# Products of the second layer's modulation tied to the VectorE split of a later weight unit, at most two pending

## The chip, the cores and the metric

The kernel runs on one core of one Trainium2 chip. The metric is the device time of one execution in microseconds (us). TensorE does the matrix products, VectorE and ScalarE work on tiles element by element, GpSimd does little here, and SyncE (SP) does nothing but issue the DMA loads of the weights.

## What is computed

A network of two layers on 256 rows of 2048 numbers, all in fp32. Each layer scales, shifts and gates with a modulation that is a product of one vector with a large matrix. The first layer's mixer is gated linear attention with a short convolution, the second's is a windowed mean with a grouped projection. Cut to what matters here:

```python
def modulation(cond, w, b, n):
    m = jax.nn.silu(cond) @ w[:, :n * D_MODEL] + b[:n * D_MODEL]
    return jnp.split(m, n, axis=-1)

for i in range(DEPTH):                                    # DEPTH = 2
    sh, sc, gt = modulation(c_lat, w_ada[i], b_ada[i], 3) # w_ada[i]: 2048 x 6144
    u = x * (1.0 + sc) + sh
    ...
    y = even_mixer(u @ w_in_e[j], ..., w_out_e[j]) if i % 2 == 0 else odd_mixer(u @ w_in_o[j], ..., w_out_o[j])
    x = layer_norm(alpha * x + gt * y, ln_g[i], ln_b[i])
```

## The kernel before

**Weights.** All weights are read once, as units of 1 MB (four tiles of 128 rows by 512 columns; `load_unit`, line 138). SyncE issues the loads one after another, and every one of them takes the next of four buffers named `raw`. So a load is issued only when what was in that buffer four loads earlier has been used. A unit is then split in two halves (`split_unit`): ScalarE casts each half to the high part `wh` (line 152), VectorE subtracts it from the raw value to get the low part `wl` (line 153). Four halves of each are kept, and some units ("wide" ones) have halves of their own, `swh` and `swl`. Each product of the network is three matmuls (lines 190 to 192): high by high, high by low, low by high. `w_next` keeps loads two units ahead of the unit in use and splits one unit ahead.

**Modulation.** The modulation's matrix (`w_ada`) comes through the same four buffers, also 1 MB at a time. The second layer's share, and the first layer's gate `gt`, are made on VectorE beside the first layer's products: for each 1 MB load four instructions (`ada_accum`, lines 532 and 534) multiply a 128x512 tile by one number of each partition and add it into a row of sums, `aacc`. When four loads are done (16 instructions), TensorE sums `aacc` over the partitions (`adaS`, line 555, or `gtb`, line 521), and VectorE adds the bias (lines 293 and 295). Such a load with its products is called a modulation load below, and the four instructions its products.

**What sets the order.** These loads and products are written by Python generators. `tick` is called for every weight unit and gives the generators a credit (so many steps per unit, a number for each stage), and `pump_ada` spends it, one `yield` per step: mostly a load with its four products. Whatever is not done when the kernel needs it is written out at once: `cols_ab` calls `pump_ada(1000)` in front of the last column block of the first layer's output projection, since the second layer's input u1 needs the whole scale and shift (A1, B1). The remaining 16 loads, those of the second layer's gate, come in the second layer. Products carry a priority; among what is ready to be placed, the scheduler orders each engine by priority, and each engine then runs its instructions in that order.

**The end of the first layer.** The output projection (`ln_blocks`) goes through four blocks of 512 columns, each with four weight units, called q0 to q3 here. Of the last block, q2 and q3 are wide. Its sums are `oacc`, one for the upper 128 rows (m=0) and one for the lower (m=1). When a half of the rows is complete, VectorE multiplies by the gate (`arow`), adds it to `xr`, takes statistics and normalises (lines 1086 to 1100 and 1156), TensorE transposes, ScalarE applies A1 and B1 (line 1164) and casts (`u1h`, line 1167), and the second layer's products (`xacc`) follow.

Of the kernel before, what the change touches and what calls it, by code (L numbers as in the profile page):

```python
# [9 lines left out]
F32 = mybir.dt.float32  # L10
# [3 lines left out]
ALU = mybir.AluOpType  # L14
# [46 lines left out]
def kernel(  # L61
# [24 lines left out]
    nc = tc.nc  # L86
    names = {}

    def nm(s):
        names[s] = names.get(s, 0) + 1  # L90
        return f"{s}_{names[s]}"
# [9 lines left out]
    @contextmanager  # L101
    def prio(offset):
        old = tc.cur_priority
        tc.cur_priority = max(0, old + offset)
        start = tc.cur_priority
        yield
        tc.cur_priority = old + tc.cur_priority - start
# [4 lines left out]
    def slot(shape, dt=F32, name="s"):  # L112
        return s4p.tile(shape, dt, tag="s4", name=nm(name))

    def mp(shape, name="mp"):
        return mpp.tile(shape, F32, tag="mp", name=nm(name))

    def acc_bank(name="acc"):
        return accp.tile([P, 512], F32, tag="acc", name=nm(name))
# [6 lines left out]
    def small(shape, name):  # L126
        return smp.tile(shape, F32, tag=name, name=nm(name))
# [15 lines left out]
    def split_unit(r, nk, wide=False):  # L143
        parts = []
        for j in range(0, nk, 2):
            w = min(2, nk - j)
            if wide:
                h, l = slot([P, w, 512], F32R, "swh"), slot([P, w, 512], F32R, "swl")
            else:
                h = whp.tile([P, w, 512], F32R, tag="wh", name=nm("wh"))  # L150
                l = wlp.tile([P, w, 512], F32R, tag="wl", name=nm("wl"))
            nc.scalar.copy(h, r[:, j : j + w, :])  # L152
            nc.vector.tensor_tensor(out=l, in0=r[:, j : j + w, :], in1=h.bitcast(F32), op=ALU.subtract)  # L153
            for i in range(w):
                parts.append((h[:, i, :], l[:, i, :]))
        return parts
# [5 lines left out]
    wst = {"l": 0, "s": 0, "u": 0}  # L162
    wraws, wparts = {}, {}

    def w_ahead(nl, ns):
        top = len(specs)
        while wst["s"] < min(top, wst["u"] + ns):
            w_load(wst["s"] + 1)
            i = wst["s"]
            with prio(-SPLIT_PRIO if n0_done[0] else -SPLIT_PRIO0):  # L170
                wparts[i] = split_unit(wraws.pop(i), specs[i][2], i in wide)
            wst["s"] = i + 1
        w_load(min(top, wst["u"] + nl))

    def w_load(n):
        while wst["l"] < n:
            i = wst["l"]
            wraws[i] = load_unit(*specs[i])
            wst["l"] = i + 1
# [136 lines left out]
    k0 = 0  # L316
# [153 lines left out]

    def pump_ada(n):
        while n > 0 and ada_bg:
            try:
                next(ada_bg[0])
                n -= 1
            except StopIteration:
                ada_bg.pop(0)

    def ada_unit(layer, k0, n0):

        if not ADA_SLOT:
            r = load_unit(w_ada[layer], k0, 4, n0)
            return [r[:, j, :] for j in range(4)]
        q = {"s": nc.sync, "g": nc.gpsimd}[ADA_SLOT]
        parts = []
        for k in (k0, k0 + 2):
            r = slot([P, 2, 512], F32, "araw")
            q.dma_start(r, w_ada[layer][k * P : (k + 2) * P, n0 : n0 + 512].rearrange("(k p) n -> p k n", p=P))
            parts += [r[:, 0, :], r[:, 1, :]]
        return parts  # L490
# [16 lines left out]
    def ada_rows_gen(layer, dst, engs):  # L507

        for nb in range(4):
            if nb % 2 == 0:  # L510
                dst.append(slot([P, 2, 512], F32, "gt"))
            g = dst[nb // 2][:, nb % 2, :]
            n0 = 2 * D + nb * 512
            nc.gpsimd.dma_start(g, b_ada[layer : layer + 1, n0 : n0 + 512].to_broadcast([P, 512]))
            a = small([P, 512], "aacc1")
            for k0 in range(0, KT, 4):
                ada_accum(ada_unit(layer, k0, n0), k0, a, engs)
                if k0 == KT - 4:
                    yield
                    pb = mp([P, 512], "gtb")  # L520
                    nc.tensor.matmul(out=pb, lhsT=ones, rhs=a, start=True, stop=True)
                    nc.vector.tensor_tensor(out=g, in0=pb, in1=g, op=ALU.add)
                    gt_done.setdefault(id(dst), set()).add(nb)
                yield

    def ada_accum(r, k0, a, engs):
        e = engs[(k0 // 4) % len(engs)]
        with prio(ADA_PRIO):
            for j in range(4):
                sc = sil[:, k0 + j, 2:3]  # L530
                if k0 + j == 0:
                    e.tensor_scalar(out=a, in0=r[j], scalar1=sc, scalar2=None, op0=ALU.mult)
                else:
                    e.scalar_tensor_tensor(out=a, in0=r[j], scalar=sc, in1=a, op0=ALU.mult, op1=ALU.add)  # L534

    def ada_cols_gen(layer, n0, dst, bias, one, engs, on_pe=()):

        for nb in range(4):
            ns = slice(4 * nb, 4 * nb + 4)
            if nb in on_pe:  # L540
                hold = []
                for _ in ada_acc_gen(layer, n0 + nb * 512, hold):
                    if not hold:
                        yield
                add_bias(dst[:, ns], to_cols(hold[0], 512)[:, :, 0], bias[:, ns], one)
                yield
                continue
            a = small([P, 512], "aacc1")
            for k0 in range(0, KT, 4):
                ada_accum(ada_unit(layer, k0, n0 + nb * 512), k0, a, engs)  # L550
                yield
            yield
            pt = mp([P, 4], "adaS")
            for q in range(4):
                nc.tensor.matmul(out=pt[:, q : q + 1], lhsT=a[:, q * P : (q + 1) * P], rhs=ones[:, 0:1], start=True, stop=True)
            add_bias(dst[:, ns], pt, bias[:, ns], one)
# [9 lines left out]
    prev, k0 = None, 0  # L566
# [31 lines left out]
    def drain(gen=None):  # L598
        while bg and (gen is None or gen in bg):
            pump(1e9 if gen is None else 1)  # L600
# [460 lines left out]
    for i in range(2):  # L1061
        n0 = i * 512
# [13 lines left out]
    def ln_blocks(src, order, getu, res, gt, budget, after, before=None, between=None, halves=False):  # L1076

        rt, accs, seen = {}, {}, {}

        def add(nb, m, cs=slice(0, 512)):  # L1080
            if nb not in rt:
                rt[nb] = res(nb)
            while ada_bg and not (len(gt) > nb // 2 and nb in gt_done.get(id(gt), ())):
                pump_ada(1)
            t = small([P, 512], "arow")[:, cs]
            nc.vector.tensor_tensor(out=t, in0=accs[nb][m + (cs.start > 0)][:, cs], in1=gt[nb // 2][:, nb % 2, cs], op=ALU.mult)
            r = rt[nb][:, m, cs]
            nc.vector.scalar_tensor_tensor(out=r, in0=r, scalar=ALPHA, in1=t, op0=ALU.mult, op1=ALU.add)
            parts = [r] if not (halves and m) or cs != slice(0, 512) else [r[:, 0:256], r[:, 256:512]]
            for v in parts:  # L1090
                nc.vector.bn_stats(out=cst[m][:, seen_st[m], :], in_=v)
                seen_st[m] += 1

        def done(m, cs, end):
            with prio(-LN_PRIO if m else 0):
                add(order[-1][0], m, cs)
                if not end:
                    return
                mv = small([P, 2], "mv")
                nc.vector.bn_aggr(out=mv, in_=cst[m][:, 0 : seen_st[m], :])  # L1100
                after(m, rt, mv[:, 0:1], mv[:, 1:2])

        seen_st = [0, 0]
        for nb, qs in order[:-1]:
            if 1 in qs:
                drain()
            if nb not in accs:
                accs[nb] = [acc_bank("oacc") for _ in range(2)]
                seen[nb] = 0
            gemm(src, nb * 512, qs, range(2), getu, accs[nb], first=seen[nb] == 0, last=seen[nb] + len(qs) == 4, budget=budget)  # L1110
            seen[nb] += len(qs)
            if seen[nb] == 4:
                for m in range(2):
                    add(nb, m)
        if before:
            before()
        nb, qs = order[-1]
        accs[nb] = [acc_bank("oacc") for _ in range(2)]
        gemm_by_tile([(src, nb * 512, qs, accs[nb], True)], getu, done, between=between, halves=halves)
        return rt  # L1120
# [181 lines left out]
    for s in ODD:  # L1302
        g = int(s[1])
        if s == "g0":
            accs = [acc_bank("xacc") for _ in range(2)]
            f = gate_evac(0)
# [81 lines left out]
```

## Time and profile before

| | |
|---|---|
| time, median of 3 runs | 1006.15 us (1005.88 to 1007.38) |
| time of the profiled execution | 1010.29 us |
| its span | 1008.5 us |
| TensorE busy | 960.9 us (95%) |
| TensorE weight loads | 759.2 us (75%) |
| VectorE busy | 801.6 us (79%) |
| ScalarE busy | 469.3 us (47%) |
| DMA | 252 GB/s over the span |

The span is the profiled execution from its first to its last instruction. Busy shares are means over all stages. A wait names what the waiting instruction got last; the engine behind it in the list waits with it, since each engine runs its own list in order.

### The profile page before, as it was taken

To read this page: it belongs to the slowest core of one execution; us is meant where nothing else is said; L and a number is where in the kernel's file an instruction comes from. 1 tells how busy PE (TensorE), PEld (TensorE's weight loads), DVE (VectorE), ACT (ScalarE), POOL (GpSimd) and SP (SyncE) were. 2 spreads that over 40 slices of the span, in tenths; PEclk is the share of its full clock that TensorE was granted. 3 is DMA by queue.
4 is the path that set the end of the run, shared out by engine and by line. 5 is a ranking of instruction groups with operands and counts; after the bars stand their busy time and mean duration, and the time that the engine had idled before them with its cause. 6 is when DMAs were issued, how large, how long until landed. Compare 5 with 4: busy or idle time off the path is not lost.

```text
span 1008.5 us, 14323 instructions
## 1 busy us (share of the span) xinstructions
PE 960.9 (95%) x5654; PEld 759.2 (75%) x5654; DVE 801.6 (79%) x1142; ACT 469.3 (47%) x643; POOL 24.4 (2%) x56
## 2 busy tenths in 40 slices
PE   5899999999999999999999899999999999989995
PEld 4566656778878877887878778888778778778885
DVE  1555546979996999779999688897979997666676
ACT  2422214356675676236454344445745555435340
POOL 2000000000000000000000000000010001000000
PEclk9999999999999999999999999999999999999998
DMA  9977889566787586867767877985497999875532
GB/s 265 329 263 262 276 284 336 193 243 231 258 302 252 188 269 219 257 206 274 241 228 234 284 255 247 353 298 207 152 368 275 304 334 322 278 266 203 174 119 83
DMA packets 150371, 255.44 MB, mean 253 GB/s; under 512 B 5078, under 2 KB 46720, under 8 KB 150304
## 3 DMA queue, kind: packets, MB, share of 16 engines
q1 hardware_dynamic: 146592, 245.13, 72.4%
q0 software_dynamic: 2896, 8.72, 2.7%
q10 hardware_dynamic: 816, 0.68, 0.3%
q8 instruction: 44, 0.72, 0.3%
q14 instruction: 23, 0.19, 0.0%
HBM read 252.41 MB, written 2.10 MB: 252 GB/s over the span
## 4 chain that ended last, share of the span: by engine, by line
PE 41%; DVE 33%; DMA 18%; issue 5%; ACT 3%; SPq 0%; DVEq 0%; ACTq 0%
DMA raw<-in_w_ada_dram 15%; DVE wl L153 11%; DVE aacc L534 9%; PE oacc L191 5%; PE oacc L192 5%; PE oacc L190 5%; DMA raw<-in_w_in_o_dram 3%; PE xacc L192 3%; PE xacc L191 3%; PE xacc L190 3%; PE ada L274 2%; PE kacc L190 2%; PE kacc L192 2%; PE kacc L191 2%; PE pr L406 1%
## 5 line engine op out<-in xcount | busy, mean ns | idle before, releaser
L152 ACT CAST wh<-raw 128x1024 fp32r<-128x1024 f32 (+1 forms) x250 | 257.0, 1044 | 252.6 <-PE xacc L192 77.9
L153 DVE TENSOR_TENSOR wl<-raw,wh 128x1024 fp32r<-128x1024 f32 (+1 forms) x250 | 297.3, 1210 | 49.3 <-ACT wh L152 47.1
L534 DVE SCALAR_TENSOR_TENSOR aacc<-raw,sil,aacc 128x512 f32<-128x512 f32 x240 | 179.0, 747 | 34.2 <-DMA raw<-in_w_ada_dram 30.7
L190 PE MATMUL xacc<-wh,uxh 128*128 128x512 f32 x384 | 153.8, 400 | 0.0
L191 PE MATMUL xacc<-wl,uxh 128*128 128x512 f32 x384 | 150.9, 393 | 0.9 <-DVE wl L153 0.9
L192 PE MATMUL xacc<-wh,uxl 128*128 128x512 f32 x384 | 151.1, 394 | 0.0
L191 PEld LDWEIGHTS xacc<-wl,uxh 128*128 128x128 f32 x384 | 72.6, 189 | 17.3 <-DVE wl L153 1.7
L190 PEld LDWEIGHTS xacc<-wh,uxh 128*128 128x128 f32 x384 | 72.5, 189 | 15.6 <-issue 0.5
L192 PEld LDWEIGHTS xacc<-wh,uxl 128*128 128x128 f32 x384 | 72.4, 188 | 15.6 <-issue 0.2
L426 DVE TENSOR_TENSOR knat<-kacc,knat 128x512 f32<-128x512 f32 x64 | 42.8, 685 | 35.8 <-PE kacc L192 35.6
L285 ACT COPY arow<-ada 128x256 f32<-128x256 f32 (+1 forms) x9 | 3.1, 349 | 101.9 <-PE ada L274 101.9
L274 PE MATMUL ada<-raw,sil 128*32 128x256 f32 (+1 forms) x576 | 36.2, 380 | 12.0 <-DMA raw<-in_w_ada_dram 12.0
L190 PE MATMUL xacc<-wh,u1h 128*128 128x512 f32 x112 | 44.8, 400 | 0.8 <-ACT u1h L1167 0.8
L190 PE MATMUL oacc<-wh,y1h 128*128 128x512 f32 (+1 forms) x120 | 45.5, 379 | 0.0
L192 PE MATMUL oacc<-wh,y1l 128*128 128x512 f32 (+1 forms) x120 | 45.0, 375 | 0.0
L191 PE MATMUL oacc<-wl,y1h 128*128 128x512 f32 (+1 forms) x120 | 45.0, 375 | 0.0
L191 PE MATMUL xacc<-wl,u1h 128*128 128x512 f32 x112 | 44.1, 394 | 0.3 <-DVE wl L153 0.3
L192 PE MATMUL xacc<-wh,u1l 128*128 128x512 f32 x112 | 44.0, 393 | 0.0
L274 PEld LDWEIGHTS ada<-raw,sil 128*32 128x32 f32 x576 | 17.0, 118 | 28.6 <-issue 12.3
L190 PE MATMUL kacc<-wh,uxh 128*128 128x512 f32 x64 | 26.8, 418 | 1.5 <-ACT uxh L398 1.5
L1228 PE MATMUL xacc<-wh,dm 128*128 128x512 f32 x64 | 26.2, 409 | 1.6 <-ACT wh L152 1.6
L190 PE MATMUL kacc<-wh,uch 128*128 128x512 f32 x64 | 26.4, 412 | 0.5 <-DVE knat L426 0.5
(339 smaller groups left out, 1865.0 us busy)
## 6 DMA issues: line engine op xcount, KB each, us to landing
raw<-in_w_ada_dram SPq DMA_DIRECT2D x96, 1024.0 KB, 6.3
raw<-in_w_in_e_dram SPq DMA_DIRECT2D x54, 1024.0 KB, 6.0
raw<-in_w_in_o_dram SPq DMA_DIRECT2D x32, 1024.0 KB, 7.1
raw<-in_w_out_e_dram SPq DMA_DIRECT2D x16, 1024.0 KB, 6.7
raw<-in_w_out_o_dram SPq DMA_DIRECT2D x16, 1024.0 KB, 5.1
raw<-in_w_in_e_dram SPq DMA_DIRECT2D x18, 512.0 KB, 7.2
raw<-in_w_pool_dram SPq DMA_DIRECT2D x4, 1024.0 KB, 7.5
gt<-in_b_ada_dram POOLq DMA_DIRECT2D x8, 256.0 KB, 3.8
```

Source lines behind the costliest of these rows:

```text
L152: nc.scalar.copy(h, r[:, j : j + w, :])
L153: nc.vector.tensor_tensor(out=l, in0=r[:, j : j + w, :], in1=h.bitcast(F32), op=ALU.subtract)
L190: nc.tensor.matmul(out=acc, lhsT=uh, rhs=wh, start=start, stop=False)
L191: nc.tensor.matmul(out=acc, lhsT=uh, rhs=wl, start=False, stop=False)
L192: nc.tensor.matmul(out=acc, lhsT=ul, rhs=wh, start=False, stop=stop)
L274: nc.tensor.matmul(out=ps[32 * g : 32 * g + 32, :], lhsT=sil[:, kt, 2 - 2 * half : 34 - 2 * half], rhs=r[:, j, :], start=half == 0 and kt ...
L285: arow_ins.append(nc.scalar.copy(a[:, :nw], ps))
L406: nc.tensor.matmul(out=pr[32 * g : 32 * g + 32, :], lhsT=wr[:, kk, :], rhs=quad_u[kk // 2][:, kk % 2, :], start=True, stop=True,)
L426: nc.vector.tensor_tensor(out=dst, in0=acc, in1=dst, op=ALU.add)
L534: e.scalar_tensor_tensor(out=a, in0=r[j], scalar=sc, in1=a, op0=ALU.mult, op1=ALU.add)
L1228: nc.tensor.matmul(out=accs[0], lhsT=dh, rhs=wh, start=f, stop=False)
```

## The change

The products of a modulation load are no longer written at the load. They are kept in a list (`put_off`), marked with the number of the weight unit that is loaded next. When `w_ahead` has split that unit, the waiting products are written behind its last VectorE subtraction (`issue_after`). At most two such groups are pending; a third one makes the oldest be written at once. Before the sums over partitions the generators now step idly as long as something is pending (`while pend: yield`), and such a step takes a step of the credit as any other does. Where everything is wanted at once (`pump_ada(1000)`, and the gate in `add`), the pending products are written out first. The products, loads, splits and matmuls are the same in kind and number.

```diff
-            nc.vector.tensor_tensor(out=l, in0=r[:, j : j + w, :], in1=h.bitcast(F32), op=ALU.subtract)
+            wl_ins.append(nc.vector.tensor_tensor(out=l, in0=r[:, j : j + w, :], in1=h.bitcast(F32), op=ALU.subtract))
...
+    pend, wl_ins = [], []
+
+    def put_off(f):
+        while len(pend) >= 2:
+            pend.pop(0)[1]()
+        pend.append((wst["l"], f))
+
+    def pend_all():
+        while pend:
+            pend.pop(0)[1]()
...
             wst["s"] = i + 1
+            while pend and pend[0][0] <= i:
+                with tc.issue_after(wl_ins[-1].ins):
+                    pend.pop(0)[1]()
...
         while n > 0 and ada_bg:
+            if n >= 500:
+                pend_all()
...
-                ada_accum(ada_unit(layer, k0, n0), k0, a, engs)
+                put_off(lambda r=ada_unit(layer, k0, n0), k0=k0, a=a: ada_accum(r, k0, a, engs))
                 if k0 == KT - 4:
                     yield
+                    while pend:
+                        yield
...
-                ada_accum(ada_unit(layer, k0, n0 + nb * 512), k0, a, engs)
+                put_off(lambda r=ada_unit(layer, k0, n0 + nb * 512), k0=k0, a=a: ada_accum(r, k0, a, engs))
+                yield
+            while pend:
                 yield
             yield
...
             while ada_bg and not (len(gt) > nb // 2 and nb in gt_done.get(id(gt), ())):
+                pend_all()
                 pump_ada(1)
```

Three places show what moves. In all of them the numbers behind names count tiles, and lines of the changed kernel stand some 14 to 20 higher (534 is 552, 966 is 986, 190 to 192 are 204 to 206, 555 is 575).

**SyncE, the loads around the last block of the first layer's output projection.** Before:

```order
L138 DMA raw_5637<-in_w_ada_dram 128x4x512
L138 DMA raw_5651<-in_w_out_e_dram 128x4x512
L138 DMA raw_5685<-in_w_out_e_dram 128x4x512
L138 DMA raw_5725<-in_w_out_e_dram 128x4x512
L138 DMA raw_5775<-in_w_out_e_dram 128x4x512
L138 DMA raw_5785<-in_w_out_e_dram 128x4x512
L138 DMA raw_5795<-in_w_in_o_dram 128x4x512
```

and now:

```order
L138 DMA raw_5601<-in_w_out_e_dram 128x4x512
L138 DMA raw_5627<-in_w_ada_dram 128x4x512
L138 DMA raw_5641<-in_w_out_e_dram 128x4x512
L138 DMA raw_5667<-in_w_ada_dram 128x4x512
L138 DMA raw_5688<-in_w_ada_dram 128x4x512
L138 DMA raw_5701<-in_w_ada_dram 128x4x512
...
L138 DMA raw_5744<-in_w_ada_dram 128x4x512
L138 DMA raw_5750<-in_w_ada_dram 128x4x512
L138 DMA raw_5775<-in_w_out_e_dram 128x4x512
L138 DMA raw_5785<-in_w_out_e_dram 128x4x512
L138 DMA raw_5795<-in_w_in_o_dram 128x4x512
```

The block's units q0 to q3 are 5685, 5725, 5775, 5785 before and 5601, 5641, 5775, 5785 now; four modulation loads are left out by "...", so ten stand in a row between q1 and q2, where there were none.

**VectorE, the splits of q1 to q3.** Before:

```order
L1088 SCALAR_TENSOR_TENSOR xr_5751<-xr_5751,arow_5753 128x512
L153 TENSOR_TENSOR wl_5768<-raw_5725,wh_5767 128x1024
L153 TENSOR_TENSOR swl_5778<-raw_5775,swh_5777 128x1024
L153 TENSOR_TENSOR wl_5772<-raw_5725,wh_5771 128x1024
L153 TENSOR_TENSOR swl_5782<-raw_5775,swh_5781 128x1024
L153 TENSOR_TENSOR swl_5788<-raw_5785,swh_5787 128x1024
```

and now:

```order
L153 TENSOR_TENSOR wl_5768<-raw_5641,wh_5767 128x1024
L153 TENSOR_TENSOR wl_5772<-raw_5641,wh_5771 128x1024
L1107 TENSOR_TENSOR arow_5675<-oacc_5511,gt_4612 128x512
L552 SCALAR_TENSOR_TENSOR aacc_10_5590<-raw_5627,sil,aacc_10_5590 128x512
...
L552 SCALAR_TENSOR_TENSOR aacc_12_5731<-raw_5738,sil,aacc_12_5731 128x512 x4
L552 SCALAR_TENSOR_TENSOR aacc_12_5731<-raw_5744,sil,aacc_12_5731 128x512 x4
L552 SCALAR_TENSOR_TENSOR aacc_12_5731<-raw_5750,sil,aacc_12_5731 128x512 x4
L309 TENSOR_TENSOR shT_139<-adaS_5756,colT 128x4
L1166 TENSOR_TENSOR B_5134<-B_5134,shT_139 128x16
L153 TENSOR_TENSOR swl_5778<-raw_5775,swh_5777 128x1024
L153 TENSOR_TENSOR swl_5782<-raw_5775,swh_5781 128x1024
```

Between the last split of q1 (wl_5772) and the first of q2 (swl_5778) stand 44 products now (eleven loads, 5627 and the ten), three instructions of the block before, the three bias additions and the row of B; before, one split of q2 stood ahead of q1's last.

**VectorE, the attention's normalised outputs y of the first layer's third head.** Before:

```order
L534 SCALAR_TENSOR_TENSOR aacc_10_4985<-raw_5082,sil,aacc_10_4985 128x512
L966 SCALAR_TENSOR_TENSOR y_4859<-po_4861,rsy_2_4885,gs_2936 128x256 x2
L966 SCALAR_TENSOR_TENSOR y_4859<-po_4872,rsy_2_4885,gs_2936 128x256
L153 TENSOR_TENSOR wl_5040<-raw_5000,wh_5039 128x1024
L153 TENSOR_TENSOR wl_5044<-raw_5000,wh_5043 128x1024
L966 SCALAR_TENSOR_TENSOR y_4859<-po_4872,rsy_2_4885,gs_2936 128x256
```

and now:

```order
L986 SCALAR_TENSOR_TENSOR y_4792<-po_4794,rsy_2_4818,gs_2878 128x256
L153 TENSOR_TENSOR wl_4970<-raw_4930,wh_4969 128x1024
L986 SCALAR_TENSOR_TENSOR y_4792<-po_4794,rsy_2_4818,gs_2878 128x256
L153 TENSOR_TENSOR wl_4974<-raw_4930,wh_4973 128x1024
L986 SCALAR_TENSOR_TENSOR y_4792<-po_4805,rsy_2_4818,gs_2878 128x256 x2
```

The product in front of the four y is gone from there; one subtraction of a weight unit stands between the first and the second y, and one more behind the second.

On TensorE, the last block ran the m=0 matmuls of q0 to q3 (48) and then the m=1 ones (48). Now it runs the m=0 and m=1 matmuls of q0 and q1 (24 and 24), the twelve small `adaS` matmuls, and then those of q2 and q3 (24 and 24).

## Rows read from the trace of the kernel before

**Rows 1.** The page: engines, busy us, share of the span, instructions.

```profile
PE 960.9 (95%) x5654; PEld 759.2 (75%) x5654; DVE 801.6 (79%) x1142; ACT 469.3 (47%) x643; POOL 24.4 (2%) x56
```

**Rows 2.** Waits: engine, tile, releaser: us in total, times, longest us.

```profile
DVE aacc L534 <- DMA raw<-in_w_ada_dram: 30.7, 12, 5.6
...
DVE aacc L532 <- DMA raw<-in_w_ada_dram: 8.2, 4, 4.1
```

**Rows 3.** Waits of TensorE alone, same columns.

```profile
PE yT L974 <- DVE y L966: 5.1, 1, 5.1
...
PE y1T L1286 <- DVE gate L1333: 3.6, 1, 3.6
```

**Rows 4.** Timeline, 567 to 584: start, us, engine, instruction, [idle before <-releaser].

```profile
567.04 0.37 SPq L138 DMA_DIRECT2D raw<-in_w_ada_dram  x1
...
570.58 0.16 DVE L295 TENSOR_TENSOR shT<-adaS,colT 128x4 f32<-128x4 f32 x1 [0.67 <-PE adaS L555]
...
580.00 0.75 DVE L534 SCALAR_TENSOR_TENSOR aacc<-raw,sil,aacc 128x512 f32<-128x512 f32 x1 [5.58 <-DMA raw<-in_w_ada_dram]
580.66 1.26 DVE L966 SCALAR_TENSOR_TENSOR y<-po,rsy,gs 128x256 f32<-128x256 f32 x3
...
575.76 0.39 PE L192 MATMUL xacc<-wh,uxl 128*128 128x512 f32 x1
581.29 0.99 PE L974 MATMUL yT<-ident,y 128*128 128x128 f32 x4 [5.14 <-DVE y L966]
...
582.93 0.63 PE L192 MATMUL xacc<-wh,uxl 128*128 128x512 f32 x1
583.35 0.63 PE L190 MATMUL xacc<-wh,uxh 128*128 128x512 f32 x1
```

**Rows 5.** Windows: busy us (x) of PE, PEld, DVE, ACT, POOL; PEclk; DMA; GB/s.

```profile
581.50:583.00 1.50, 1.50 (x7) 1.22 (x6) 1.50 (x4) 0.67 (x2) 0.00 (x0) 0.50 0.03 11
...
682.00:688.00 6.00, 6.00 (x29) 4.95 (x28) 3.49 (x8) 0.00 (x0) 0.00 (x0) 1.00 1.04 395
```

**Rows 6.** Timeline, 885 to 889: the second layer's gate on VectorE and TensorE.

```profile
885.73 0.75 DVE L534 SCALAR_TENSOR_TENSOR aacc<-raw,sil,aacc 128x512 f32<-128x512 f32 x1 [4.74 <-DMA raw<-in_w_ada_dram]
886.39 1.22 DVE L153 TENSOR_TENSOR wl<-raw,wh 128x1024 fp32r<-128x1024 f32 x1
887.53 1.22 DVE L1333 TENSOR_TENSOR gate<-gate,pooled 128x1024 f32<-128x1024 f32 x1
```

**Rows 7.** Timeline, VectorE in the output projection: products in a row, then between others.

```profile
634.08 3.11 DVE L534 SCALAR_TENSOR_TENSOR aacc<-raw,sil,aacc 128x512 f32<-128x512 f32 x4
...
653.44 0.74 DVE L534 SCALAR_TENSOR_TENSOR aacc<-raw,sil,aacc 128x512 f32<-128x512 f32 x1
654.10 2.35 DVE L153 TENSOR_TENSOR wl<-raw,wh 128x1024 fp32r<-128x1024 f32 x2
```

**Rows 8.** Timeline, last block: SyncE, TensorE, VectorE, ScalarE.

```profile
657.14 16.39 SPq L138 DMA_DIRECT2D raw<-in_w_out_e_dram  x5
...
676.60 0.40 PE L190 MATMUL oacc<-wh,ybh 128*128 128x512 f32 x1
...
682.08 0.39 PE L190 MATMUL oacc<-swh,yah 128*128 128x512 f32 x1
...
700.38 0.39 PE L192 MATMUL oacc<-swh,yal 128*128 128x512 f32 x1
700.62 0.39 PE L190 MATMUL xacc<-wh,u1h 128*128 128x512 f32 x1
...
677.90 1.22 DVE L153 TENSOR_TENSOR wl<-raw,wh 128x1024 fp32r<-128x1024 f32 x1
...
687.72 0.69 DVE L1086 TENSOR_TENSOR arow<-oacc,gt 128x512 f32<-128x512 f32 x1 [2.48 <-PE oacc L192]
...
689.90 0.26 DVE L1100 BATCH_NORM_AGGREGATE mv<-cst 128x2 f32<-128x24 f32 x1
...
695.72 0.62 ACT L1167 CAST u1h<-uf 128x512 fp32r<-128x512 f32 x1
```

## The prediction

> **What bounds the kernel now.** I read the engines' busy times first. TensorE is busy 960.9 us of a span of 1008.5 [rows 1], so all its idle time together is 47.6 us, and nothing that VectorE does costs anything unless TensorE has to wait for it. Next the waits. VectorE stands 30.7 us in 12 waits and 8.2 us in 4 at a product whose load has not landed, 38.9 us in all [rows 2]; these are the waits that the change is aimed at, since a product placed behind the split of a later load finds its own load landed. Then TensorE's own waits, to see how many of those 38.9 us arrive there: two places. One is 5.1 us at yT, the other 3.6 us at y1T [rows 3]. Everywhere else TensorE has enough queued while VectorE stands. So the most there is to win is some 9 us with their after-effects, and the question is what the moved products do to TensorE elsewhere.
>
> The sum is made against the profiled execution, 1010.29 us, and carried over to the median of the runs, 1006.15, by taking the same 4.1 us off.
>
> **The gain at yT.** A modulation load is issued at 567.04 and its last product starts at 580.00, and VectorE's four y stand behind it; TensorE has run out at 576.0 (its last matmul starts at 575.76) and gets yT at 581.29 [rows 4]. In the change's order no product stands there; one subtraction of a weight unit stands between the y. Its unit was cast by about the time TensorE ran out, and it takes about 1.2 us (the same operation at 886.39 [rows 6]), so I put yT 1.4 us behind 576.1 instead of 5.1: 3.7 us gained. After the wait the clock stood at 0.50, the lower of the two levels, 1.2 GHz [rows 5], and matmuls came 0.42 us apart (582.93 to 583.35 [rows 4]) where they come 0.228 apart at full clock (24 from 676.60 to 682.08 [rows 8]). Some 8 of them, 8 x 0.19 = 1.6 us, of which I count 1.0. Bounds: nothing, if the subtraction is as late as the load was, and 5.1 + 1.6 = 6.7.
>
> **The gain at y1T.** VectorE stands 4.74 us at a product until 885.73, then subtracts (1.22) and multiplies the gate (1.22), and then TensorE goes on [rows 6]. The gate comes out of TensorE's own last sums by an activation, so that and its multiplication remain; I keep 2.1 of the 3.6 us, a gain of 1.5 between bounds of 0 and 2.5. Together 6.2, between 0 and 9.2. The other 14 waits at products cost TensorE nothing now, so taking them away gains nothing.
>
> **The loss at the last block of the output projection.** The idle steps before each sum use up credit, so the modulation falls behind, and what is missing at the last block is written at once: ten loads between the loads of q1 and q2, and 44 products on VectorE between the splits of q1 and q2. Both engines' lists are run in order, so q2's low parts wait for all of them. From the start of the block's first matmul, called e (676.60):
> - q1's last split ends at e + 2.5 (677.90 + 1.22 [rows 8]). It was held by ScalarE's cast, which waited for TensorE, and that stays.
> - One product behind another that adds to the same row takes 0.78 us (four from 634.08 to 637.19), one between others 0.66 (653.44 to 654.10) [rows 7]. About half of the 44 stand in each way: 22 x 0.78 + 22 x 0.66 = 31.7 us; bounds 44 x 0.66 = 29.0 and 44 x 0.78 = 34.3.
> - Three instructions of the block before, some 0.6 each (one arow takes 0.69 [rows 8]): 1.8 us. The last bias waits for TensorE's small matmuls, 0.67 + 0.16 [rows 4], and B comes behind it; with the earlier two in part, 2.5 us (bounds 1 and 3).
> - The first split of q2, 1.2 us. It ends at e + 2.5 + 31.7 + 1.8 + 2.5 + 1.2 = e + 39.7.
>
> TensorE has the 48 matmuls of q0 and q1 as cover, 48 x 0.228 = 10.9 us. So VectorE gets some 12 products done under cover, and TensorE stands from about e + 12 to e + 39.7, some 28 us in one piece. Two matmuls of q2 need only its high part; the other 46 then take 10.5 us, so the block's last one starts at e + 50.2. Before it started at e + 23.8 (700.38 [rows 8]). That is **26.4 us** lost, and 1.6 us more at the lower clock behind the wait, as at yT.
>
> For the loads: four products use up a buffer every 2.6 to 3.1 us, which asks for a megabyte in that time, some 350 to 395 GB/s. The trace has 395 GB/s over a stretch of 6 us [rows 5], so I take VectorE as the pace. The bound above is from the five loads issued in 16.39 us [rows 8], (16.39 - 0.37)/4 = 4.0 us each: four loads are in the buffers when the products begin, the other seven come 1.1 us late each, + 8 us. The Trainium skill, "DMA: Bandwidth & Descriptors", § Bandwidth, gives 341 GB/s for transfers of this size; by that estimate a load takes 3.1 us and nothing changes in the sum but its last microsecond or two.
>
> **The loss behind the block.** Before, the layer norm of m=0 ran beside the 48 matmuls of m=1: from m=0's first arow at 687.72 to the cast of u1h, ending at 696.34, with TensorE at work until 700.6 [rows 8]. In the new order only 24 matmuls, 5.5 us, are left behind m=0's last, and m=1's addition stands ahead of m=0's statistics, so these start some 0.7 us after TensorE's last matmul. From the aggregate (689.90) to the end of u1h (696.34) are 6.4 us [rows 8]. So the next layer's first matmul, which followed at once (700.62), comes 7 us later. Bounds: 3.3 (8.8 us of norm from the end of m=0, less the 5.5) and 12 (the second half's norm is late as well, another 5). One more fall of the clock, 0.8 (bounds 0 and 1.6). **7.8 us.**
>
> **The second layer.** The 16 loads of its gate keep their places among SyncE's loads, and each one's products move behind a split. Its other waits of TensorE are short and of other causes, so 0, bounds -1 and +2.
>
> **The sum.** 26.4 + 1.6 + 7.8 - 6.2 = + 29.6 us: 1039.9 for an execution such as the profiled one, **1036** on the footing of the median.
>
> **Rivals.**
> - *The waits go and nothing is paid (faster).* If VectorE came to q2's split before TensorE had run through q0 and q1, within 10.9 us, only the gain would be left: 1006.15 - 6.2 = 1000, 997 at best. It is decided by the number of products between the two splits: at most 12 fit, and 44 stand there. For it speaks only that the trace of before never shows the products late at this point. 3 in 100.
> - *Nothing changes.* VectorE's work is the same to the instruction, and TensorE's too. If only sums of work counted, the time would stay at 1006. Against it speaks that TensorE now needs a low part behind 44 instructions, with 10.9 us in hand. 3 in 100. By the Trainium skill, "Perfetto Trace Analysis", § Identifying the Most-Contended Engine, one looks for the engine with the most busy time, TensorE's by its weight loads; that would be VectorE (79% against 75%), whose work is not touched, so the rule gives no change. The waits at yT and y1T say that the order counts beside the sum.
> - *Partly hidden.* If TensorE reached the block late or the following layer took back what its queue had saved up, half of the 34 us would go: 1010 to 1022. Only a few microseconds of waits stand in the second layer to be taken back, the largest of them y1T's 3.6 us [rows 3]. 8 in 100.
> - *The ten loads are the pace.* At 4.0 us per load the stop is 8 us longer, 1044, and with the layer norm at its upper bound 1049. For it speaks that other loads landed late alone (13 us for the one of 567.04 [rows 4]), against it the 395 GB/s. 12 in 100.
>
> **How the numbers follow.** Forecast 74 in 100, and the rivals 3, 3, 8 and 12. All products at 0.66 take 2.7 off the forecast, the layer norm at its lower bound 3.7, no loss of clock 2.4, the gains at their upper bound 3.0: 1024. The upper ends, with no gain at all (6.2) and the layer norm's 5 more, make 1047. The range of 1021 to 1048 takes in the edge of the partly hidden case and the lower half of the slow loads. About 2 us, 0.2%, can be told from no change: faster 0.03, within it 0.03, slower 0.94.
>
> **What would show it.** In the profile of the changed kernel TensorE has one wait of 25 to 30 us at the first q2 matmul that takes a low part (or the adaS in front of it), with VectorE busy through it with aacc, and a second one of some 7 us at the next layer's first xacc. VectorE's waits for w_ada loads fall well below 38.9 us, yT's wait to 1 or 2 and y1T's to about 2. The prediction is wrong if VectorE stands waiting for loads in that stop (then the loads are the pace), if the stop is under 15 us, or if yT waits as long as before.

## The result, and the profile after

The changed kernel takes 1051.3 us (median of 4, 1048.4 to 1054.5) where the kernel before takes 1006.0 (1005.9 to 1007.4): a ratio of 1.045, interval 1.041 to 1.048. It is 45 us slower. The forecast was 30 us slower, and its range ended at 1048, so the direction was right and the size was not.

The page of the kernel after (engines as in [rows 1], and the group of the products) shows the same work as before, with VectorE now waiting only 3.5 us in all in front of this group:

```profile
span 1048.0 us, 14326 instructions
...
PE 969.2 (92%) x5654; PEld 764.5 (73%) x5654; DVE 805.2 (77%) x1142; ACT 472.7 (45%) x645; POOL 24.4 (2%) x56
...
L552 DVE SCALAR_TENSOR_TENSOR aacc<-raw,sil,aacc 128x512 f32<-128x512 f32 x240 | 178.3, 749 | 3.5
```

TensorE's waits after (total, times, longest), to be held against [rows 3]:

```profile
PE adaS L575 <- DVE aacc L552: 25.7, 3, 10.4
...
PE gtb L539 <- DVE aacc L552: 8.3, 5, 3.1
PE xacc L1249 <- ACT dm L1205: 4.8, 1, 4.8
...
PE y1T L1307 <- DVE gate L1354: 2.3, 1, 2.3
...
PE yT L994 <- DVE y L986: 0.4, 1, 0.4
```

The two waits that were to go have shrunk as forecast: yT from 5.1 to 0.4 us, y1T from 3.6 to 2.3. In their place stand 25.7 us at the sums of the modulation, adaS, which sit in the last block of the output projection, and 8.3 us at the gate's sums, gtb, where the kernel before had 0.3. The last block's timeline after, TensorE first and then VectorE (start, duration, [idle before]):

```profile
662.71 1.02 PE L575 MATMUL adaS<-ones,aacc 128*128 128x1 f32 x8
...
669.16 0.39 PE L204 MATMUL oacc<-wh,ybh 128*128 128x512 f32 x1
...
679.82 0.39 PE L206 MATMUL oacc<-wh,ybl 128*128 128x512 f32 x1
687.35 1.87 PE L575 MATMUL adaS<-ones,aacc 128*128 128x1 f32 x8 [7.14 <-DVE aacc L552]
697.40 1.84 PE L575 MATMUL adaS<-ones,aacc 128*128 128x1 f32 x8 [8.19 <-DVE aacc L552]
709.60 1.87 PE L575 MATMUL adaS<-ones,aacc 128*128 128x1 f32 x8 [10.36 <-DVE aacc L552]
...
713.07 0.80 PE L205 MATMUL oacc<-swl,yah 128*128 128x512 f32 x1 [0.54 <-DVE swl L153]
...
725.46 0.39 PE L206 MATMUL oacc<-swh,yal 128*128 128x512 f32 x1
...
731.96 0.50 PE L204 MATMUL xacc<-wh,u1h 128*128 128x512 f32 x1 [1.10 <-ACT u1h L1188]
...
750.62 0.80 PE L1249 MATMUL xacc<-wh,dm 128*128 128x512 f32 x1 [4.76 <-ACT dm L1205]
...
671.56 1.22 DVE L153 TENSOR_TENSOR wl<-raw,wh 128x1024 fp32r<-128x1024 f32 x1
...
679.52 0.48 DVE L550 TENSOR_SCALAR aacc<-raw,sil 128x512 f32<-128x512 f32 x1 [0.60 <-DMA raw<-in_w_ada_dram]
679.92 8.03 DVE L552 SCALAR_TENSOR_TENSOR aacc<-raw,sil,aacc 128x512 f32<-128x512 f32 x12
689.25 0.16 DVE L309 TENSOR_TENSOR shT<-adaS,colT 128x4 f32<-128x4 f32 x1 [1.29 <-PE adaS L575]
...
699.28 0.16 DVE L309 TENSOR_TENSOR shT<-adaS,colT 128x4 f32<-128x4 f32 x1 [1.36 <-PE adaS L575]
699.36 10.19 DVE L552 SCALAR_TENSOR_TENSOR aacc<-raw,sil,aacc 128x512 f32<-128x512 f32 x13
711.51 0.16 DVE L309 TENSOR_TENSOR shT<-adaS,colT 128x4 f32<-128x4 f32 x1 [1.96 <-PE adaS L575]
...
711.80 4.63 DVE L153 TENSOR_TENSOR swl<-raw,swh 128x1024 fp32r<-128x1024 f32 x4
```

TensorE finishes q0 and q1 at 680 and has little but three groups of small sums to do until q2's low part comes at 713 (a group is four matmuls in the program and eight in the records). VectorE goes through the 37 products that are still left of the 44 in that time, in rows of up to 13. The granted clock was 0.67 and 0.65 in these two windows (columns as in [rows 5]), so for part of the time it stood at the lower of its two levels, 1.2 GHz.

```profile
675.00:700.00 25.00, 8.91 (x39) 7.53 (x38) 21.43 (x34) 0.00 (x0) 0.00 (x0) 0.67 0.89 306
700.00:725.00 25.00, 14.86 (x53) 11.87 (x54) 20.53 (x26) 7.98 (x8) 0.00 (x0) 0.65 0.94 321
```

The next mark is the first product of the pooled part, xacc<-wh,dm. Before, it stood at

```profile
715.05 0.39 PE L1228 MATMUL xacc<-wh,dm 128*128 128x512 f32 x1
```

With that the two profiled executions can be set side by side (us):

| stretch | before | after | difference | forecast |
|---|---|---|---|---|
| start to the last block's first matmul | 676.60 | 669.16 | -7.4 | -4.7 |
| that to the block's last matmul | 23.8 | 56.3 | +32.5 | +28.0 |
| that to the first xacc<-wh,dm | 14.7 | 25.2 | +10.5 | +7.8 |
| that to the end of the span | 293.4 | 297.4 | +3.9 | -1.5 |
| sum | 1008.5 | 1048.0 | +39.5 | +29.6 |

In a second profile of the kernel before the four stretches are 673.9, 23.8, 14.7 and 295.7 us, so 2 to 3 us in the first and the last row differ from one execution of the same kernel to the next.

One more pair of rows had changed that the forecast didn't look at. These are the waits of VectorE's splits for ScalarE's casts, and of those casts for weight loads, after:

```profile
DVE wl L153 <- ACT wh L152: 99.7, 60, 8.9
...
ACT wh L152 <- DMA raw<-in_w_in_o_dram: 40.8, 17, 7.9
...
ACT wh L152 <- DMA raw<-in_w_in_e_dram: 23.4, 9, 7.1
ACT wh L152 <- DMA raw<-in_w_out_e_dram: 20.2, 5, 7.5
```

Of VectorE's 38.9 us at loads of products [rows 2] 0.6 us are left, but its splits now wait 99.7 us for casts, where they waited 47.1. That is what the experiments below follow up.

### The profile page after: what moved, and what is told of

The parts are those of the page before. It is cut to its first block, busy times and chain, and to the rows that moved or that the text cites. A ratio compares the mean times of both kernels' runs of the same rounds, so it can differ in the third digit from the quotient of the medians.

```text
span 1048.0 us, 14326 instructions
## 1 busy us (share of the span) xinstructions
PE 969.2 (92%) x5654; PEld 764.5 (73%) x5654; DVE 805.2 (77%) x1142; ACT 472.7 (45%) x645; POOL 24.4 (2%) x56
## 4 chain that ended last, share of the span: by engine, by line
PE 59%; DVE 19%; DMA 14%; ACT 4%; issue 4%; SPq 0%; ACTq 0%; DVEq 0%
DVE wl L153 7%; PE xacc L204 7%; PE xacc L206 7%; PE xacc L205 7%; DVE aacc L552 5%; DMA raw<-in_w_in_o_dram 5%; DMA raw<-in_w_ada_dram 4%; PE oacc L205 4%; PE oacc L206 4%; PE oacc L204 4%; ACT wh L152 2%; PE kacc L204 2%; DMA raw<-in_w_in_e_dram 2%; PE kacc L206 2%; PE kacc L205 2%
## 5 line engine op out<-in xcount | busy, mean ns | idle before, releaser
L153 DVE TENSOR_TENSOR wl<-raw,wh 128x1024 fp32r<-128x1024 f32 (+1 forms) x250 | 298.6, 1214 | 103.5 <-ACT wh L152 99.7
L152 ACT CAST wh<-raw 128x1024 fp32r<-128x1024 f32 (+1 forms) x250 | 256.9, 1047 | 268.1 <-PE xacc L206 71.9
L440 DVE TENSOR_TENSOR knat<-kacc,knat 128x512 f32<-128x512 f32 x64 | 42.9, 688 | 34.4 <-PE kacc L206 34.2
L288 PE MATMUL ada<-raw,sil 128*32 128x256 f32 (+1 forms) x576 | 36.0, 378 | 11.0 <-DMA raw<-in_w_ada_dram 10.9
L288 PEld LDWEIGHTS ada<-raw,sil 128*32 128x32 f32 x576 | 16.9, 117 | 27.5 <-issue 12.0
L575 PE MATMUL adaS<-ones,aacc 128*128 128x1 f32 x64 | 10.4, 283 | 25.8 <-DVE aacc L552 25.7
L152 ACT CAST swh<-raw 128x1024 fp32r<-128x1024 f32 x16 | 16.3, 1048 | 39.5 <-DMA raw<-in_w_out_e_dram 37.7
```

The source lines that it names most:

```text
L153: wl_ins.append(nc.vector.tensor_tensor(out=l, in0=r[:, j : j + w, :], in1=h.bitcast(F32), op=ALU.subtract))
L288: nc.tensor.matmul(out=ps[32 * g : 32 * g + 32, :], lhsT=sil[:, kt, 2 - 2 * half : 34 - 2 * half], rhs=r[:, j, :], start=half == 0 and kt ...
L440: nc.vector.tensor_tensor(out=dst, in0=acc, in1=dst, op=ALU.add)
```

## Experiments

Theory A: the idle steps make the modulation late, and the ten loads left over at the last block, with their 44 products, cost the time. Rival B: the products' new places cost time by themselves. Rival C: the stop's pace is set by the loads, not by VectorE.

**The kernel before, profiled again.** No edit.

> The kernel before, profiled a second time, for the footing of the forecast: the first profile took 1010.3 us where the timed runs take 1006. If the 13 us landing of the load in front of yT belonged to that one execution, yT waits under 2 us here and the time is 1005 to 1007, and then there was little to gain at yT. If it belongs to the order of the loads, yT waits 4 to 6 us again and the execution takes about 1010.

Measured: 1009.8 us in this execution, and yT waited 3.2 us, y1T 2.6. Neither of the two expectations fits well: some of yT's 5.1 us belonged to the first execution, but a wait is there again. The timed runs of the kernel before, here and in the next comparisons, lay between 1003 and 1012, so a profiled 1010 is within the ordinary spread.

**The put-off alone.** After the change, with

```diff
-            while pend:
-                yield
+            pend_all()
             yield
```

and the same in the generator of the gate.

> The products are put off as in the change, but no idle steps are taken: what is pending is written just before the sum over partitions, so the modulation's loads keep their places of before and none are left at the last block. Theory A (the idle steps make the modulation late, the clump of ten loads costs the time): no stop of TensorE at the last block, 999 to 1009 us. Rival B (the products' new places themselves cost, since sums wait for products placed behind later splits): 1015 us or more, with adaS and gtb waits of TensorE of over 10 us spread over the program.

Measured: 1022.0 us (1019.5 to 1024.5) against 1008.1, a ratio of 1.013 (1.010 to 1.016). No stop at the last block, but 14 us lost, against A. The time is one that B had, but not for B's reason: the waits of TensorE at adaS and gtb together are under 6 us, where B asked for over 10. The rows that had grown are again the casts' waits for weight loads; of the put-off alone:

```profile
DVE wl L153 <- ACT wh L152: 81.6, 52, 5.5
...
ACT wh L152 <- DMA raw<-in_w_in_o_dram: 34.2, 11, 11.2
ACT wh L152 <- DMA raw<-in_w_out_e_dram: 33.2, 10, 6.1
ACT wh L152 <- DMA raw<-in_w_in_e_dram: 26.5, 11, 5.6
```

and of the kernel before, profiled again:

```profile
DVE wl L153 <- ACT wh L152: 48.4, 36, 4.1
...
ACT wh L152 <- DMA raw<-in_w_in_o_dram: 24.5, 11, 8.6
ACT wh L152 <- DMA raw<-in_w_in_e_dram: 14.9, 3, 7.4
...
ACT wh L152 <- DMA raw<-in_w_out_e_dram: 3.6, 1, 3.6
```

The timeline shows one such place. The same two loads of the output projection in the kernel before (second profile), with the products in front of them on VectorE and the cast behind:

```profile
591.57 2.32 DVE L534 SCALAR_TENSOR_TENSOR aacc<-raw,sil,aacc 128x512 f32<-128x512 f32 x3
...
593.92 2.64 SPq L138 DMA_DIRECT2D raw<-in_w_out_e_dram  x2
...
602.82 1.05 ACT L152 CAST wh<-raw 128x1024 fp32r<-128x1024 f32 x1 [2.97 <-PE xacc L192]
...
603.98 0.39 PE L190 MATMUL oacc<-wh,ybh 128*128 128x512 f32 x1
```

and with the put-off alone:

```profile
597.10 3.11 DVE L551 SCALAR_TENSOR_TENSOR aacc<-raw,sil,aacc 128x512 f32<-128x512 f32 x4
...
600.23 3.00 SPq L138 DMA_DIRECT2D raw<-in_w_out_e_dram  x2
...
607.46 2.01 ACT L152 CAST wh<-raw 128x1024 fp32r<-128x1024 f32 x2 [6.07 <-DMA raw<-in_w_out_e_dram]
...
605.49 0.39 PE L204 MATMUL oacc<-wh,ybh 128*128 128x512 f32 x1
```

In both, the first weight load is issued within 0.05 us of the end of the products: they were the last to use the buffer that this load takes. Put off, they end 6.3 us later, so the load is issued 6.3 us later. Of these 6.3 us, 1.5 are a lag of the whole kernel at that point (the output projection's first matmul starts at 603.98 and at 605.49), and 4.8 remain. A cast that had waited for TensorE now waits 6 us for its data. Hence theory D: a product that is put off holds its buffer longer, and the load that takes that buffer next comes late. At the start it was said to be the load four places on; that isn't always so. In the kernel before the products shown belong to the load issued at 581.36 (the next modulation load, of 589.87, landed only at 597.01), and the load that they release, at 593.92, is the third behind it. Rival E keeps to the order on VectorE.

**The idle steps alone.** The kernel before with

```diff
+            for _ in range({0: 5, 1: 4, 3: 1}.get(nb, 0) if one else int(nb == 0)):
+                yield
             yield
```

and one such step for each of the first three sums of the gate, which are the idle steps that the change takes ahead of the last block.

> The kernel before with the idle steps alone, 14 of them at the same places as in the change; every product stays at its load. Ten loads then stand between those of q1 and q2 again, with 39 products between the splits. Theory A: 1040 to 1050 us, a stop of TensorE of 25 to 30 us at the last block. Rival B: 1004 to 1010 us, as the placement is that of before.

Measured: 1038.8 us (1035.8 to 1040.7) against 1008.1, ratio 1.030 (1.027 to 1.033): 31 us, a little under A's 1040, with a stop of 25.4 us (676.5 to 701.9) where A put it (two of the three sums, since here the first one still fell under cover):

```profile
PE adaS L559 <- DVE aacc L536: 20.8, 2, 10.5
...
PE xacc L1232 <- ACT dm L1188: 4.7, 1, 4.7
```

The two parts make up the whole: 1.013 x 1.030 = 1.044, and the change has 1.045. The change's idle steps in the second layer are in neither part. The stretches of the profiled executions (us) show where each part acts:

| stretch | before (two profiles) | put-off alone | idle steps alone | change |
|---|---|---|---|---|
| start to the last block's first matmul | 676.6, 673.9 | 683.8 | 665.5 | 669.2 |
| that to the block's last matmul | 23.8, 23.8 | 23.8 | 51.3 | 56.3 |
| that to the first xacc<-wh,dm | 14.7, 14.7 | 14.7 | 25.4 | 25.2 |
| that to the end of the span | 293.4, 295.7 | 300.5 | 295.5 | 297.4 |

The idle steps make the way to the last block 8 to 11 us shorter (ten loads and their products no longer stand in it) and lose 27.5 in the block and 11 behind it. The put-off loses 7 to 10 us ahead of the block and 5 to 7 in the second layer. In the change both act at once.

**Fewer products in the stop.** After the change, with one product of four in nine of the loads:

```diff
-            for j in range(4):
+            for j in range(1 if few[0] else 4):
```

> The changed kernel with one product of four in nine of the loads at the last block; 27 products are left out, so the second layer's shift and part of its scale are not complete. 17 products instead of 44 stand between the splits of q1 and q2. If VectorE is the pace of the stop (A), it is 27 x 0.72 = 19 us shorter and the time some 1030 us. If the loads are the pace (rival C), the stop keeps its length within 5 us and the time is 1044 to 1050. If both are near each other, the loads take over at once: 12 loads at 2.7 us from the first of the ten, 32 us, a stop of some 20 us, 1036 to 1040.

Measured: 1043.6 us in one execution. The stop between q1 and q2 is 22.8 us (680.1 to 702.9) where it was 31.1 (680.2 to 711.3), so VectorE had been its pace; then the loads take over, as in the third expectation. The time lies above its 1036 to 1040: the stretch from the block's last matmul to the first xacc<-wh,dm took 28.2 us where the change took 25.2. The products now wait for the loads, and come 2.7 us apart, 388 GB/s for the megabyte:

```profile
693.74 0.75 DVE L556 SCALAR_TENSOR_TENSOR aacc<-raw,sil,aacc 128x512 f32<-128x512 f32 x1 [2.10 <-DMA raw<-in_w_ada_dram]
696.45 0.75 DVE L556 SCALAR_TENSOR_TENSOR aacc<-raw,sil,aacc 128x512 f32<-128x512 f32 x1 [1.96 <-DMA raw<-in_w_ada_dram]
699.15 0.75 DVE L556 SCALAR_TENSOR_TENSOR aacc<-raw,sil,aacc 128x512 f32<-128x512 f32 x1 [1.95 <-DMA raw<-in_w_ada_dram]
```

So even with fewer products a stop remains: ten loads at 2.7 us take 27 us, and the matmuls of q0 and q1 cover 10.9 us of them.

**Five buffers, before and with the put-off alone.** For D against E, one more buffer for the loads and no other edit:

```diff
-NSLOT = 31
+NSLOT = 30
...
-    wraw = ctx.enter_context(tc.tile_pool(name="wraw", bufs=4))
+    wraw = ctx.enter_context(tc.tile_pool(name="wraw", bufs=5))
```

> The kernel before with five buffers for the loads instead of four (paid for with one 4 KB slot of 31): the footing for the next run. Theory D (in the change a product that is put off keeps its buffer longer, and the weight load that waits for that buffer is issued late) says little about this one: VectorE's waits at products get shorter, 998 to 1008 us. If the lost slot costs, up to 1015.

> The put-off products without idle steps, with five buffers for the loads. Theory D: with a buffer to spare the late products hold nothing up, and the 14 us that the same kernel lost with four buffers shrink to 5 or less against the kernel before with five buffers; ScalarE's casts wait less than 20 us for w_out_e loads (33 us with four). Rival E (it is the order on VectorE and the sums that stand too early on TensorE, not the buffers): it stays 10 to 16 us slower than the kernel before with five.

Measured, on one chip: the kernel before with five buffers 994.3 us (991.8 to 996.3), the put-off with five 990.8 (989.8 to 991.5). With four buffers the put-off costs 14 us, with five it gains 3.5 (the ranges of the four runs just do not meet). This is what D asked for and not what E did. The casts' waits of the put-off with five:

```profile
ACT wh L152 <- DMA raw<-in_w_in_e_dram: 18.1, 7, 7.4
ACT wh L152 <- DMA raw<-in_w_in_o_dram: 11.6, 4, 3.8
ACT wh L152 <- DMA raw<-in_w_out_e_dram: 11.3, 3, 5.4
```

The w_out_e row is 11.3 us where it was 33.2, the w_in_o row 11.6 where it was 34.2.

Two things limit this pair of runs. The edit doesn't change the buffers alone, since the scheduler places the instructions anew: VectorE's 1142 instructions run in the same order in both profiles of the kernel before, and with five buffers only some 670 of them line up with that order. And the kernel before with five came out below its 998 to 1008, not for the reason given: VectorE's waits at loads of products are still 36.3 us, while the casts' waits for the loads of w_in_e, w_in_o and w_out_e fell from 43.0 us to 27. So the next run, with four buffers, counts for D beside this one.

**A shorter put-off, four buffers.** As the put-off alone, with the products marked for the next split that is made:

```diff
-        pend.append((wst["l"], f))
+        pend.append((wst["s"], f))
```

> No idle steps, four buffers, and each product put behind the next split that is made rather than that of a unit loaded later, so that it is used up after 0.95 later loads on average (0.58 before, 1.61 when it is put off as in the change). Theory D: the loss follows the time for which a buffer is held, 4 to 6 us of the 14 remain, 1008 to 1014 us; if the waits of VectorE at products fall as well, down to 1002. Rival E: a product behind a split costs whichever split it is, 1016 to 1022 us.

Measured: 1004.4 us (10 runs, 1000.8 to 1009.0), ratio 0.997 (0.995 to 0.999). This is better than D's first figure and near its second: held shorter, the buffers cost no more than the removed waits give back. The casts' waits for the three kinds of weight loads are 52.4 us here, 93.9 with the longer put-off and 43.0 in the kernel before (second profile), and VectorE waits for no load in front of a product. E's 1016 to 1022 is out. How the two effects divide these 3 us stays open.

**The put-off in the second layer alone.** The first layer as before:

```diff
+                if layer == 1:
+                    put_off(lambda r=ada_unit(layer, k0, n0), k0=k0, a=a: ada_accum(r, k0, a, engs))
+                else:
+                    ada_accum(ada_unit(layer, k0, n0), k0, a, engs)
```

> Only the products of the second layer's gate are put off; all of the first layer is as before. In the profile of the kernel with everything put off and no idle steps, some 5 us of its 14 came in the second layer. If these parts add up, 1010 to 1014 us, with a wait of TensorE at gtb; if they don't, within 2 us of the kernel before.

Measured: 1014.7 us (8 runs, 1010.5 to 1019.4), ratio 1.007 (1.004 to 1.010): 7 us, a little more than the 5 expected. The second layer was not free of cost. But these 7 us aren't simply a part of the 14: this kernel keeps the change's idle steps in front of the second layer's gtb sums, and the put-off alone has none. In the profiles the stretch behind the first xacc<-wh,dm is 299.3 us here, 300.5 in the put-off alone, and 293.4 and 295.7 in the kernel before, so the put-off costs 5 to 7 us there without idle steps as well.

**The change, and the shorter put-off, with five buffers.**

> The changed kernel as it is, with five buffers for the loads. If the two costs are separate (idle steps with their clump of ten loads, some 31 us; held buffers, some 14 us), the second goes and the first stays, since the 44 products still stand between the splits of q1 and q2: 990.8 + 31 = 1022 us, 1016 to 1028. If the clump's stop also came from the buffers (the loads as its pace), 1000 to 1012.

> No idle steps, each product behind the next split, five buffers. Theory D: with a buffer to spare it no longer matters for how long a product holds its own, so this is within 3 us of the products put off behind a later unit's split with five buffers, 988 to 994 us. If the longer put-off is worth something of its own (VectorE waits less at products), it is 3 to 6 us slower than that, near the kernel before with five buffers.

Measured: the change with five buffers 1026.2 us (1024.1 to 1028.5), 35 us above the put-off without idle steps. The two ran on different chips, but their ratios to the kernel before, each on its own chip, say the same: 1.018 (1.013 to 1.023) and 0.984 (0.981 to 0.987). So the clump's cost does not go away with a buffer to spare, as the separate costs have it. Across chips, the fifth buffer takes 25 us off the change and 13 off the kernel before; the 12 us between them are near the 14 of the put-off alone. The shorter put-off with five 993.8 us (991.0 to 994.4), within 3 us of the longer one, as D has it; but it also lies near the kernel before with five (994.3), so these runs do not say what the length is worth.

Of all kernels here, the put-off without idle steps on five buffers is the fastest, 990.8 us: a ratio to the kernel before of 0.984 (0.981 to 0.987). Most of that, 13 us, comes with the fifth buffer and without the put-off (0.987, 0.983 to 0.991).

## Why the prediction was off

- **The place and kind of the loss: right.** One stop in the last block, VectorE busy through it with products, and no wait for loads between the splits of q1 and q2 but 0.6 us. Idle steps alone cost 31 us. The forecast's terms for them were 26.4 + 1.6 + 7.8 = 35.8 us for 44 products, or 32 for the 39 that stand there in that run (5 x 0.72 less).
- **The put-off itself: the step that failed.** It was costed as a gain of 6.2 us alone, with the other fourteen waits of VectorE at nothing and the second layer at 0. The waits did shrink. What was left out is that a product is also what frees a buffer for a later load, and that can be one of a weight, as the w_out_e load shown above. With four buffers the put-off costs 14 us by itself, and by the ratios as much on top of the idle steps (1.045 to 1.030). So the put-off was 20 us too cheap and the idle steps 5 us too dear, which is the 15 us between 1036 and 1051. How much of the loss is the held buffers' alone isn't measured: TensorE's waits at gtb, 8.3 us in the change (4.3 of them in the second layer) and 3.9 in the put-off alone, are sums that stand and wait for products placed later, as rival B had it.
- **The block's terms: too small by 4.5 us** (+32.5 for 28.0; this and the next three go by the profiled stretches). The last split of q1 ended 3.6 us behind the block's start (671.56 + 1.22 - 669.16) for 2.5. The bias additions waited 1.3, 1.4 and 2.0 us for the sums, 4.6 together, where 2.5 were put for everything at that place: with the clock at its lower level (granted 0.50 from 687.30 to 689.20) a group of sums took 1.87 us, and the additions behind them stop VectorE itself. The 44 products were sized well, though 7 of them were done under the cover of q0 and q1 and not 12. q2's first split ended 43.8 us behind the start (39.7 forecast), 3.2 of the 4.1 us explained by the split and the additions and 0.6 by the one wait for a load.
- **Behind the block: too small by 2.7 us.** The first xacc came 6.5 us behind the block's last matmul (7 forecast). The wait of 4.8 us at dm had been named as the upper bound, the second half's norm coming late as well, and not taken.
- **Up to the last block: -7.4 for -4.7, and near by luck.** It was forecast as the gain at yT. What was measured is a gain of the idle steps, which move three groups of sums and their loads from there into the stop (8 to 11 us in their own run), less a loss of the put-off (7 to 10 in its own run).
- **The second layer: +3.9 for -1.5** in the profile (+1.7 against the second profile of the kernel before).
- **The footing.** The 4.1 us between the first profile and the median were taken off the forecast as if every profiled execution had them. The profile after lies 1.5 us below its own median instead. On the profiles' footing the forecast was 1039.9 for a measured 1049.8, so 9.9 of the 15 us are in the four stretches (4.5 + 2.7 + 5.4 - 2.7) and the rest here.
- **The range.** Its upper end, 1047, took in two of the sum's upper bounds, no gain and the layer norm's 5 us. With those of the products (2.6), the additions (0.5), the clock (0.8) and the second layer (2) it would have been 1053.
- **The rivals.** Loads as the pace was wrong for the change (VectorE waited 0.6 us for them between the splits) and right as the next bound, with a stop 8 us shorter; the loads came 2.7 us apart there, for the rival's 4.0 and the 3.1 of the estimate beside it. The demand of the products was put a little too narrow there: a megabyte in 2.64 to 3.12 us is 336 to 397 GB/s, for 350 to 395. "Nothing changes" fell, and with it the rule of the Trainium skill, "Perfetto Trace Analysis", § Identifying the Most-Contended Engine, as a guide for this change: VectorE's busy time stayed the same within 4 us while the time grew by 45. The same page of the Trainium skill, § Optimization Strategy, says that a gap that keeps repeating on the engine that should be saturated can mean too few buffers. The run with a fifth buffer is in line with it, 13 us, though the waits here were scattered and the order on VectorE changed with the buffer.

## What to carry to other kernels

Before a use is moved later, ask what else it releases: in a set of buffers that go round the last use of one transfer is the start of another, and a wait taken off VectorE can come back as a late load for ScalarE and a late split for VectorE. An idle step in a generator that is paid from a budget of steps delays all that follows, and the rest falls due at once at the next hard deadline; count what is left there, and how much of it fits under the work that covers it. One buffer more is a cheap way to tell a cost of order from a cost of holding, but look whether the order stayed the same; a shorter hold with the same buffers tells it too.

## What the runs showed of the hardware

In the run with fewer products, loads of a megabyte in a row landed 2.7 us apart, 388 GB/s, with nothing but the loads to wait for. In the changed kernel one group of sums (eight matmuls of 128x1 in the records) took 1.87 us at 687.35, where TensorE had stood for 7.1 us and the granted clock was 0.50, the lower level (687.30 to 689.20). A group took 1.02 us at 662.71, behind matmuls without a gap, where the granted clock was 1.00 (662.70 to 663.60).
